# A decoder step on one core: four stores moved behind the first key evacuation, two sums of squares behind the first weight tiles

## The chip, the cores and the metric

One core of a Trainium2 chip runs the whole program. The time is device microseconds of one execution; "before" is the median of three runs. The engines are TensorE (PE, with its weight loads as PEld), VectorE (DVE), ScalarE (ACT), GpSimd (POOL) and SyncE (SP). SP issues most loads, ACT issues some loads and stores, each in the order of its own instruction stream.

## The reference, cut to what matters

The reference is one decoder layer over 512 prompt rows and 32 sample rows of width 1024: a hybrid mixer (mLSTM heads and differential attention), cross-attention to 256 memory rows, and a gated ConvFFN. The change lies in the opening, where the keys of the memory rows are made and the prompt rows are normed for the mixer's input projection:

```python
def rms_norm(x, g):
    y = xf * lax.rsqrt(jnp.mean(xf * xf, axis=-1, keepdims=True) + RMS_EPS)
    return (y * g.astype(jnp.float32)).astype(x.dtype)

def mem_kv(mem, g_mem_src, w_mk, w_mv):
    mn = rms_norm(mem, g_mem_src)
    mk = (mn @ w_mk).reshape(B, MEM_TOKENS, MEM_HEADS, MEM_HEAD_DIM)
    mv = (mn @ w_mv).reshape(B, MEM_TOKENS, MEM_HEADS, MEM_HEAD_DIM)
    return mk, mv
...
    h = rms_norm(x, g_mix_pre)
    z = h @ w_in
```

## The kernel before

**Products.** A float32 operand is split into a high part (cast to fp32r, on ACT) and a low part (the difference, on DVE or POOL: `split`, lines 146 and 147). A product is three matmuls: high x high, high x low weight, low x high weight (lines 407 to 409 for 512 columns, line 465 for the heads in two column halves). Each weight tile of 512 KB is loaded by SP into a staging buffer `wst` and split into `wslot`, of which four buffers exist. The eight tiles of `w_mk` share the low part between DVE and POOL (`split_w`, lines 221 and 223); the other tiles leave it to DVE.

**The memory rows.** Two blocks `xm` of 128 rows are loaded. `norm_turn` transposes each on PE (line 328, `tp`), multiplies it with the gain on DVE (line 330, `ht`), and splits it into `memT` (ACT line 146, POOL for the first four column tiles and DVE for the others, line 147). The row norm is not applied here: the scale 1/rms of each row (`mrs`) comes from a sum of squares on ACT (`sumsq`, line 309), two small POOL operations (`rstd`, lines 302 and 304) and a copy on DVE (line 523). It is multiplied in only when the keys leave PSUM.

**The keys.** `mem_k` makes the keys in two column halves `i`. In each, `gemmA` walks over eight tiles of 128 rows of the contraction (one step of the generator each) for both row blocks, 48 matmuls per half, and then `ev` takes each block out of PSUM: scale on ACT (line 531, `mkv`), store, four transposes on PE (line 535, `mkt`), copy and second store on ACT (lines 537 and 538). 

**The prompt rows.** The loop over `mem_k` (lines 575 to 580) puts the input norm of the five row blocks between its steps: load `xb` (line 568), sum of squares on ACT, POOL, scaling on DVE (line 318, `hN`), transposes on PE, `ht` on DVE, split into `hT` (ACT, and POOL for the first four column tiles, DVE for the others). Blocks 0 to 3 are prompt rows, block 4 the sample rows. After the keys, `gemmB` makes the four mLSTM key heads (line 465), first columns 0 to 255 (blocks 0 and 1) of all heads, then the rest, and takes them out on ACT (line 637). The gate products (lines 658 and 659) follow.

**The stores.** The products `ht` of the memory rows (`kept`, four tiles of 128 x 512) are stored to a scratch array `mem_d` by ACT (line 583), to be loaded again for the memory values (line 545, about 314 us into the span). In the text their stores stand behind the `mem_k` loop.

**What sets the order.** The text gives priorities, not the order: a scheduler orders each engine's instructions by its own estimate of when they become ready. `tc.issue_after(x)` makes what stands under it wait, in that order, for instruction `x`. The program uses eight completion counters for the DMAs of SP and ACT, given out in turn; a DMA's issue waits until the DMA eight before it, which had the same counter, has landed.

Of the kernel before, what the change touches and what calls it, by code (L numbers as in the profile page):

```python
# [15 lines left out]
P = 128  # L16
DM = 1024
# [60 lines left out]
def kernel(ctx: ExitStack, tc: tile.TileContext, I, O):  # L78
    nc = tc.nc
# [25 lines left out]
    def N(name, w=1024):  # L105
        return npool.tile([P, 1032], F32, name=name, tag="N")[:, :w]

    def T2(shape, name, dt=F32):
        return t2p.tile(list(shape), dt, name=name, tag="T2")

    def Z(name):
        return zp.tile([P, 512], F32, name=name, tag="Z")

    def at(name="at"):
        return psa.tile([P, 512], F32, name=name, tag="at")

    def mmp(name="mm"):
        return psm.tile([P, 512], F32, name=name, tag="mm")

    def small(w, name, p=P):  # L120
        return sm.tile([p, w], F32, name=name, tag=name)
# [5 lines left out]
    def v2(t, b):  # L127
        return t.rearrange("p (a b) -> p a b", b=b)
# [7 lines left out]
    VCP = nc.vector.tensor_copy  # L136
# [12 lines left out]
    def rows(b):  # L149
        return (b * P, P) if b < 4 else (SEQ, NS)  # L150
# [29 lines left out]
    xms = [N("xm") for _ in range(2)]  # L180
# [16 lines left out]
    mrs = cst.tile([P, 2], F32, name="mrs")  # L197
# [11 lines left out]
    def stage():  # L209
        return stg.tile([P, 1024], F32, name="wst", tag="st")  # L210
# [87 lines left out]
    def rstd(ss, n, w, dim, name="rs"):  # L298

        r = small(w, name)  # L300
        if dim is not None:
            nc.gpsimd.tensor_scalar(out=r[:n], in0=ss, scalar1=1.0 / dim, scalar2=EPS, op0=MUL, op1=ADD)
            ss = r[:n]
        GTT(out=r[:n], in0=ss, in1=mhalf[:n, :w], op=ALU.pow)  # L304
        return r[:n]

    def sumsq(x, n, junk, name="ssq"):
        ss = small(1, name)
        ACT(out=junk, in_=x, func=AF.Square, accum_out=ss[:n])  # L309
        return ss[:n]  # L310
# [10 lines left out]
    def norm_turn(h, n, gname, xt, c0, pool=(True, False)):  # L321

        tmps = []
        for q in range(2):
            ps = at("tp")
            pv = v2(ps, P)[:, :, :n]
            for j in range(4):
                tr(pv[:, j, :], h[:, (4 * q + j) * P:(4 * q + j + 1) * P], ident[:n, :n])
            tmp = T2([P, 4, n], "ht")
            VTT(out=tmp, in0=pv, in1=gcol(gname, 4 * q, 4 * q + 4).unsqueeze(2).broadcast_to([P, 4, n]), op=MUL)  # L330
            put(xt, q, 0, 4, c0, n, tmp, nc.gpsimd if pool[q] else None)
            tmps.append(tmp)
        return tmps

    def norm_T(x, n, gname, xt, c0):
        norm_turn(norm_rows(x, n), n, gname, xt, c0)
# [176 lines left out]
    mem_d = dram.tile([P, 8, 256], F32, name="mem_d")  # L513
# [5 lines left out]
    W.nslots = 2  # L519
    W.pump()  # L520
    kept = [norm_turn(xms[b], P, "g_mem_src", memT, b * P) for b in range(2)]
    for b in range(2):
        VCP(out=mrs[:, b:b + 1], in_=rstd(sumsq(xms[b], P, N("hN")), P, 1, DM))
    W.nslots = NSLOT
    W.pump()
    def mem_k():
        dst = O["p_mem_k"][0, 0].rearrange("t h d -> t (h d)")
        for i in range(2):
            def ev(b, ps):
                t = Z("mkv")  # L530
                nc.scalar.mul(out=t, in_=ps, mul=mrs[:, b:b + 1])
                nc.scalar.dma_start(out=dst[b * P:(b + 1) * P, 512 * i:512 * i + 512], in_=t)
                pt = at("mkt")
                for j in range(4):
                    tr(pt[:, j * P:(j + 1) * P], t[:, j * P:(j + 1) * P], ident)
                u = Z("mkT")
                nc.scalar.copy(out=u, in_=pt)
                nc.scalar.dma_start(out=mk_d[:, 4 * i:4 * i + 4, b * P:(b + 1) * P], in_=v2(u, P))
            yield from gemmA(memT, 8, [0, 1], ev)
# [26 lines left out]
    def h_in(b):  # L566
        xbs[b] = N("xb")[:rows(b)[1]]
        dma(out=xbs[b], in_=x_in(b))
# [4 lines left out]
    VTS(out=gT[:, 36:40], in0=gT[:, 36:40], scalar1=1.0 - LAM_INIT, scalar2=None, op0=MUL)  # L573
    h_in(HB[1])
    for i, _ in enumerate(mem_k()):
        if i in HSTEPS:
            j = HSTEPS.index(i)
            norm_T(xbs[HB[j]], rows(HB[j])[1], "g_mix_pre", hT, rows(HB[j])[0])
            if j + 2 < 5:
                h_in(HB[j + 2])  # L580
    for b in range(2):
        for q, t in enumerate(kept[b]):
            nc.scalar.dma_start(out=mem_d[:, 4 * q:4 * q + 4, b * P:b * P + P], in_=t)


    masks = T2([P, MASK_W], "masks")
# [67 lines left out]
    for c0, c1 in HALF:  # L654
        n = c1 - c0
        ps = mmp()
# [3 lines left out]
        t = T2([64, n], "gt")  # L660
# [47 lines left out]
    ps = at("gtp")  # L708
# [3 lines left out]
    ps = at("gtp")  # L712
# [190 lines left out]
    ps = at("npt")  # L903
# [7 lines left out]
    for g in range(2):  # L911
        for h in range(0, H, 2):
            t = stage().rearrange("p (j b e) -> p j b e", j=2, b=4)
# [27 lines left out]
    ps = at("nT0")  # L941
# [10 lines left out]
    t = None  # L952
    for h in range(H):
        with burst(t):
            t = mm(pg[NS * h:NS * h + NS, P:2 * P + 1], lhsT=sm_t[:, h, :], rhs=vNs[:, h, :], start=True, stop=True).ins
    for h in range(H):
        with burst(t):
            t = mm(pg[NS * h:NS * h + NS, 4:12], lhsT=qT[:, h, SEQ:], rhs=nT[:, h, :], start=True, stop=True).ins
    for b in range(NB):
        for h in range(H):  # L960
            with burst(t):
                t = mm(pi[NS * h:NS * h + NS, 0:P], lhsT=qzm[:, 256 * h + b * NS:256 * h + (b + 1) * NS],
                       rhs=csts[b // 4, h][:, b % 4, :], start=(b == 0), stop=(b == NB - 1)).ins
# [12 lines left out]
    ps = at("nTt")  # L976
# [317 lines left out]
    ps = at("dat")  # L1294
# [114 lines left out]
    def mk_turn(i):  # L1409
        b, c = i // 2, i % 2  # L1410
        if c == 0:
            kts[b] = wp.tile([P, 8, 256], F32, name="kT", tag="W")
        for q in range(2):
            ps = at("tpk")
            for j in range(4):
                t = tr(ps[:, j * P:(j + 1) * P], kst[i][:, (4 * q + j) * P:(4 * q + j + 1) * P], ident)
            (VCP if q else nc.scalar.copy)(out=kts[b][:, 4 * q:4 * q + 4, c * P:(c + 1) * P], in_=v2(ps, P))
        return t.ins

    def mk_scores(b):  # L1420
        ps = mmp("ssc")[:, :256]
        for c in range(2):
            for h in range(H):
                t = mm(ps[NS * h:NS * h + NS], lhsT=qs[:, 2 * h + c], rhs=kts[b][:, 2 * h + c, :], start=(c == 0), stop=(c == 1))
        sample_exp(sall, b, ps, nm, su)
        return t.ins
# [35 lines left out]
    for b in range(4):  # L1462
        t = mk_scores(b)
    with tc.issue_after(t):
        for j in range(8, 16):
            t = mk_turn(j)
# [7 lines left out]
    with tc.issue_after(t):  # L1474
        for b in range(4, NB):
            t = mk_scores(b)
# [20 lines left out]
    ps = at("ost")  # L1497
    for e in range(2):
        tr(ps[:, e * P:(e + 1) * P], oS[:, e * P:(e + 1) * P], ident)
    ps = ps[:, :256].rearrange("p (e h n) -> p h e n", e=2, n=NS)  # L1500
# [20 lines left out]
    for t0 in (0, 4):  # L1521
        ps = at("cvp")
# [5 lines left out]
    ps = at("cvp")  # L1528
# [145 lines left out]
    for gi, js in enumerate(groups):  # L1674
# [8 lines left out]
        def one(b, ps, i, s, cs=slice(0, 512)):  # L1683
            t = act[i // 2][:, i % 2]
            st, en = i == 0, i == nk - 1
            if b == 4:
                return sample_mm(ps, [acs[i], acs[i + 1]], s[1], i == 0, i == nk - 2)
            s = s[0]
            c0 = b * P
            mm(ps, lhsT=t[:, 0, c0:c0 + P], rhs=s[:, 0, i % 2, cs], start=st, stop=False)  # L1690
            mm(ps, lhsT=t[:, 0, c0:c0 + P], rhs=s[:, 1, i % 2, cs], start=False, stop=False)  # L1691
            return mm(ps, lhsT=t[:, 1, c0:c0 + P], rhs=s[:, 0, i % 2, cs], start=False, stop=en)  # L1692
# [29 lines left out]
        if not last:  # L1722
            behind = []
            for n0 in (0, 512):
# [3 lines left out]
                ps = [mmp() for _ in range(4)]  # L1728
                for i in range(nk):
# [3 lines left out]
                    for b in range(4):  # L1733
                        t = one(b, ps[b], i, s)
# [5 lines left out]
            ps = {n0: at("sdn") for n0 in (0, 512)}  # L1740
# [8 lines left out]
        def chunk(b, n0):  # L1749
            while len(wd) < (nk // 2 if n0 == 0 else nk):  # L1750
                wd.append(W.get())
            w = 256 if (b, n0) == (TORD[-1], 512) else 512
            for o in range(0, 512, w):
                ps = mmp()[:, :w]
                for i in range(0, nk, 2 if b == 4 else 1):
                    t = one(b, ps, i, wd[(n0 and nk // 2) + i // 2], slice(o, o + w))
                add_y(b, ps, n0 + o, w)
            return t
# [39 lines left out]
        t = chunk(TORD[1], 0)  # L1798

        for n0 in (0, 512):  # L1800
            with burst(t.ins):
                t = chunk(TORD[0], n0)
# [77 lines left out]
```

## Time and profile before

| what | value |
|---|---|
| median of 3 runs | 958.01 us |
| the three runs | 953.81, 958.01, 958.31 us |
| the profiled execution | 956.79 us |
| its span, first to last instruction | 955.0 us |
| its mean granted TensorE clock | 0.993 |

In the rows of the timeline the first number is the start, the second the duration, both in us; what ended the idle time before an instruction stands in brackets. "SPq" and "ACTq" are DMA issues of those engines. In a list of waits the numbers are total, times and longest. Matmuls overlap in the pipeline, so that a single 128x512 matmul lasts 0.39 us in the list while one starts every 0.23 us.

### The profile page before, as it was taken

What the parts mean: (1) busy time and instruction counts of PE and PEld (TensorE: products, weight loads), DVE (VectorE), ACT (ScalarE), POOL (GpSimd) and SP (SyncE); (2) the same over time, 40 slices, a digit from 0 to 9 for tenths busy, and PEclk for the clock granted to TensorE, in tenths of its full rate; (3) what the DMA queues carried; (4) which work ended last, traced back from release to release, by engine and by line L of the source; (5) the groups of instructions that cost most, each with busy time, mean ns of one, the idle gap of its engine ahead of it and who ended that gap; (6) DMA issues with size and microseconds to landing.
All of it is one profiled execution on the core that took longest, in us unless ns stands there. A gap on an engine that the chain in (4) does not pass through costs nothing. (4 is left out here: it accounts for less than half of the span.)

```text
span 955.0 us, 17088 instructions
## 1 busy us (share of the span) xinstructions
PE 932.7 (98%) x6619; PEld 810.6 (85%) x6619; DVE 599.2 (63%) x1129; ACT 388.8 (41%) x750; POOL 197.5 (21%) x383
## 2 busy tenths in 40 slices
PE   8999999999999999999999999999999999999995
PEld 5899777879866778998777799989988997999974
DVE  5745144565887448635654769727758676676867
ACT  5655133344676447624544523332212222222232
POOL 6610000024432217300000444001110110111114
PEclk9999999999999999999999999999999999999998
DMA  8950023334825429955953743063053302512023
GB/s 278 309 184 2 1 89 136 89 110 150 264 90 183 155 94 329 307 155 167 353 213 114 206 134 89 4 177 89 4 144 79 122 26 79 165 48 89 24 92 116
DMA packets 120674, 130.27 MB, mean 136 GB/s; under 512 B 8568, under 2 KB 86233, under 8 KB 120593
## 3 DMA queue, kind: packets, MB, share of 16 engines
q1 hardware_dynamic: 114408, 125.69, 41.9%
q10 hardware_dynamic: 6184, 3.48, 1.2%
q8 instruction: 52, 0.85, 0.4%
q14 instruction: 30, 0.24, 0.1%
HBM read 112.22 MB, written 16.93 MB: 135 GB/s over the span
## 5 line engine op out<-in xcount | busy, mean ns | idle before, releaser
L146 ACT CAST wslot<-wst 128x1024 fp32r<-128x1024 f32 x125 | 130.9, 1050 | 259.9 <-issue 74.7
L477 PE MATMUL mm<-fT,wslot 128*128 128x256 f32 x1872 | 235.9, 288 | 0.0
L477 PEld LDWEIGHTS mm<-fT,wslot 128*128 128x128 f32 x1872 | 234.4, 188 | 1.8 <-issue 0.8
L147 DVE TENSOR_TENSOR wslot<-wst,wslot 128x1024 fp32r<-128x1024 f32 x125 | 155.1, 1245 | 89.3 <-ACT wslot L146 88.8
L1691 PE MATMUL mm<-wslot,act 128*128 128x512 f32 (+1 forms) x180 | 70.2, 391 | 0.0
L1692 PE MATMUL mm<-wslot,act 128*128 128x512 f32 (+1 forms) x180 | 70.0, 392 | 0.0
L1690 PE MATMUL mm<-wslot,act 128*128 128x512 f32 (+1 forms) x180 | 69.3, 387 | 0.0
L1598 POOL COPY cvo<-u 128x2 f32<-128x2 f32 x43 | 11.0, 256 | 204.8 <-DVE u L1596 194.7
L407 PE MATMUL mm<-wslot,hT 128*128 128x512 f32 x128 | 52.2, 408 | 0.0
L409 PE MATMUL mm<-wslot,hT 128*128 128x512 f32 x128 | 51.5, 403 | 0.0
L408 PE MATMUL mm<-wslot,hT 128*128 128x512 f32 x128 | 51.3, 401 | 0.0
L477 PE MATMUL mm<-hT,wslot 128*128 128x256 f32 (+1 forms) x384 | 51.0, 289 | 0.0
L1593 DVE TENSOR_TENSOR u<-mm,rsb 128x256 f32<-128x256 f32 x43 | 18.2, 424 | 51.0 <-PE mm L477 50.1
L477 PEld LDWEIGHTS mm<-hT,wslot 128*128 128x128 f32 x384 | 49.2, 188 | 0.5 <-issue 0.2
L1690 PEld LDWEIGHTS mm<-wslot,act 128*128 128x128 f32 x180 | 34.3, 191 | 8.0 <-issue 0.8
L1691 PEld LDWEIGHTS mm<-wslot,act 128*128 128x128 f32 x180 | 33.8, 188 | 7.2
L1692 PEld LDWEIGHTS mm<-wslot,act 128*128 128x128 f32 x180 | 33.8, 188 | 7.2 <-issue 0.4
L1610 ACT ACTIVATE c<-c 128x560 f32<-128x560 f32 x21 | 14.1, 672 | 56.7 <-DVE c L1604 56.7
L1604 DVE SCALAR_TENSOR_TENSOR c<-u,cvT,c 128x560 f32<-128x560 f32 x43 | 34.3, 798 | 0.9
L1603 DVE SCALAR_TENSOR_TENSOR c<-u,cvT,c 128x560 f32<-128x560 f32 x43 | 34.1, 793 | 0.2
L1703 DVE TENSOR_TENSOR yp<-mm,yp 128x512 f32<-128x512 f32 (+1 forms) x41 | 27.2, 674 | 5.1 <-PE mm L1692 5.0
L409 PEld LDWEIGHTS mm<-wslot,hT 128*128 128x128 f32 x128 | 24.5, 191 | 5.3
(474 smaller groups left out, 1857.7 us busy)
## 6 DMA issues: line engine op xcount, KB each, us to landing
wst<-in_w_up_dram SPq DMA_DIRECT2D x42, 512.0 KB
wst<-in_w_in_dram SPq DMA_DIRECT2D x28, 512.0 KB
wst<-in_w_down_dram SPq DMA_DIRECT2D x20, 512.0 KB
wst<-in_cache_mem_k_dram SPq DMA_DIRECT2D x16, 512.0 KB
wst<-in_w_mk_dram SPq DMA_DIRECT2D x8, 512.0 KB
xb<-in_x_prompt_dram SPq DMA_DIRECT2D x8, 512.0 KB
wst<-in_cache_dk_dram SPq DMA_DIRECT2D x16, 256.0 KB
wst<-in_cache_dv_dram SPq DMA_DIRECT2D x16, 256.0 KB
```

Source lines behind the costliest of these rows:

```text
L146: nc.scalar.copy(out=hi, in_=src)
L147: (eng or nc.vector).tensor_tensor(out=lo, in0=src, in1=f32(hi), op=SUB)
L407: mm(ps[b], lhsT=xt.hi(k, c0, c0 + n), rhs=s[:, 0, kk, :], start=(k == 0), stop=False)
L408: mm(ps[b], lhsT=xt.hi(k, c0, c0 + n), rhs=s[:, 1, kk, :], start=False, stop=False)
L409: return mm(ps[b], lhsT=xt.lo(k, c0, c0 + n), rhs=s[:, 0, kk, :], start=False, stop=(k == nk - 1))
L477: mm(ps[i], lhsT=s[:, l, k, :], rhs=x(k, c0, c1), start=(k == 0 and j == 0), stop=(k == 7 and j == 2))
L1603: STT(out=c, in0=u[:, 1:EXT - 1], scalar=w[1], in1=c, op0=MUL, op1=ADD)
L1604: STT(out=c, in0=u[:, 0:EXT - 2], scalar=w[0], in1=c, op0=MUL, op1=ADD)
L1690: mm(ps, lhsT=t[:, 0, c0:c0 + P], rhs=s[:, 0, i % 2, cs], start=st, stop=False)
L1691: mm(ps, lhsT=t[:, 0, c0:c0 + P], rhs=s[:, 1, i % 2, cs], start=False, stop=False)
L1692: return mm(ps, lhsT=t[:, 1, c0:c0 + P], rhs=s[:, 0, i % 2, cs], start=False, stop=en)
L1703: VTT(out=y, in0=ps, in1=y, op=ADD)
```

## The change

The sums of squares of the memory rows, with what makes `mrs` of them, go into a function that is called in the loop over `mem_k` at step 3, half-way through the first column half. The four stores to `mem_d` keep their place in the text and now wait for the second evacuation of `mem_k` (block 1 of the first column half).

```diff
     kept = [norm_turn(xms[b], P, "g_mem_src", memT, b * P) for b in range(2)]
-    for b in range(2):
-        VCP(out=mrs[:, b:b + 1], in_=rstd(sumsq(xms[b], P, N("hN")), P, 1, DM))
     W.nslots = NSLOT
     W.pump()
+    def mem_rms():
+        for b in range(2):
+            VCP(out=mrs[:, b:b + 1], in_=rstd(sumsq(xms[b], P, N("hN")), P, 1, DM))
+    evm = []
...
-                nc.scalar.mul(out=t, in_=ps, mul=mrs[:, b:b + 1])
+                evm.append(nc.scalar.mul(out=t, in_=ps, mul=mrs[:, b:b + 1]))
...
     for i, _ in enumerate(mem_k()):
+        if i == 3:
+            mem_rms()
         if i in HSTEPS:
...
-    for b in range(2):
-        for q, t in enumerate(kept[b]):
-            nc.scalar.dma_start(out=mem_d[:, 4 * q:4 * q + 4, b * P:b * P + P], in_=t)
+    with tc.issue_after(evm[1].ins):
+        for b in range(2):
+            for q, t in enumerate(kept[b]):
+                nc.scalar.dma_start(out=mem_d[:, 4 * q:4 * q + 4, b * P:b * P + P], in_=t)
```

The scheduler makes a new order of it on all five engines. Lines behind the change are numbered up to 9 higher (535 for 531, 539 for 535, 592 for 583). First ACT, at the splits of the memory rows; `memT0` is the high part of the turned rows, `wslot_119` the first weight tile, `ht` the turned rows times the gain. Before:

```order
L221 CAST wslot_119<-wst_118 128x1024
L146 CAST memT0_138<-ht_136 128x4x128
L583 DMA mem_d_115<-ht_136 128x4x128
L146 CAST memT0_138<-ht_147 128x4x128
L309 ACTIVATE hN_176,ssq_177<-xm_90 128x1024
L583 DMA mem_d_115<-ht_147 128x4x128
L146 CAST memT0_138<-ht_156 128x4x128
L221 CAST wslot_126<-wst_125 128x1024
L583 DMA mem_d_115<-ht_156 128x4x128
L146 CAST memT0_138<-ht_165 128x4x128
```

And with the change:

```order
L221 CAST wslot_119<-wst_118 128x1024
L146 CAST memT0_138<-ht_136 128x4x128
L146 CAST memT0_138<-ht_147 128x4x128
L221 CAST wslot_126<-wst_125 128x1024
L146 CAST memT0_138<-ht_156 128x4x128
L146 CAST memT0_138<-ht_165 128x4x128
L221 CAST wslot_170<-wst_169 128x1024
```

The stores and the sums have left, and the second tile (`wslot_126`) is now cast ahead of block 1 (`ht_156`, `ht_165`). POOL follows: its half of `wslot_126` stands ahead of the low part of block 1, where the two small operations of the sum stood.

Second PE, from the last key product to the first head products; `tp_292` and `tp_301` are the transposes of block 1, `tp_349` and `tp_358` of block 2, `hT00` and `hT10` the high and low part of the first four column tiles of the normed rows, `mm_577` and `mm_603` the first two heads. Before (rows that repeat are left out):

```order
L328 MATMUL tp_301<-cpk_87,hN_285 128x128 x4
L409 MATMUL mm_392<-wslot_337,memT1_139 128x512
L465 MATMUL mm_577<-hT00_244,wslot_406 128x256
L465 MATMUL mm_577<-hT10_245,wslot_406 128x256
L328 MATMUL tp_349<-cpk_87,hN_342 128x128 x4
L328 MATMUL tp_358<-cpk_87,hN_342 128x128 x4
L535 MATMUL mkt_372<-cpk_87,mkv_369 128x128 x4
```

With the change:

```order
L409 MATMUL mm_392<-wslot_337,memT1_139 128x512
L328 MATMUL tp_292<-cpk_87,hN_285 128x128 x4
L328 MATMUL tp_301<-cpk_87,hN_285 128x128 x4
L328 MATMUL tp_349<-cpk_87,hN_342 128x128 x4
L328 MATMUL tp_358<-cpk_87,hN_342 128x128 x4
L539 MATMUL mkt_372<-cpk_87,mkv_369 128x128 x4
L465 MATMUL mm_577<-hT00_230,wslot_406 128x256
L465 MATMUL mm_603<-hT00_230,wslot_448 128x256
L465 MATMUL mm_577<-hT10_231,wslot_406 128x256
```

The transposes of block 1 have gone from among the key products to behind them, next to those of block 2 and ahead of the first head product, which reads both blocks 0 and 1.

Third ACT, around the same place; `wslot_492` and `wslot_509` are the eleventh and twelfth weight tile, `xb_310` the rows of block 3, `xb_367` the sample rows, `ht_297` and `ht_306` block 1. Before:

```order
L146 CAST hT00_244<-ht_297 128x4x128
L146 CAST wslot_448<-wst_447 128x1024
L309 ACTIVATE hN_342,ssq_343<-xb_259 128x1024
L146 CAST wslot_492<-wst_491 128x1024
L146 CAST hT01_255<-ht_306 128x4x128
L309 ACTIVATE hN_410,ssq_411<-xb_310 128x1024
L146 CAST wslot_509<-wst_508 128x1024
```

With the change:

```order
L146 CAST wslot_492<-wst_491 128x1024
L146 CAST wslot_509<-wst_508 128x1024
L309 ACTIVATE hN_410,ssq_411<-xb_310 128x1024
L309 ACTIVATE hN_458,ssq_459<-xb_367 32x1024
L146 CAST hT00_230<-ht_297 128x4x128
L146 CAST hT01_241<-ht_306 128x4x128
L541 COPY mkT_377<-mkt_372 128x512
L535 ACTIVATE mkv_380<-mm_197,mrs_112 128x512
L592 DMA mem_d_115<-ht_136 128x4x128
```

The casts of block 1 stand behind the twelfth tile and two sums now, and the first store behind `mkv_380`, the second evacuation. Behind the gate products each engine's order is the one before.

## Prediction

> **What bounds the kernel now.** I read the page first: one core, and TensorE (PE) is busy almost all the time.
>
> ```profile
> span 955.0 us, 17088 instructions
> PE 932.7 (98%) x6619; PEld 810.6 (85%) x6619; DVE 599.2 (63%) x1129; ACT 388.8 (41%) x750; POOL 197.5 (21%) x383
> ```
>
> So a change that removes no matmul gains only where PE stands still. Where that is, and for whom, says the list of waits of PE, which also has the two waits of the later input norm.
>
> ```profile
> PE mm L409 <- POOL memT L147: 1.2, 2, 0.6
> PE tp L328 <- DMA xm<-in_mem_prompt_dram: 1.0, 1, 1.0
> PE tp L328 <- DVE hN L318: 0.9, 2, 0.6
> ```
>
> These are the only waits of the opening that are not the warm-up: 3.1 us. Third, the table by stage, cut at the first key product (9.46), at the first product of the mLSTM key heads (35.44) and at the first gate product (65.34). Its columns are the stretch, then busy time (and instructions) of PE, weight loads, DVE, ACT and POOL, granted clock, DMA share, GB/s.
>
> ```profile
> 9.46:14.00 4.54, 3.31 (x15) 2.16 (x14) 4.41 (x7) 3.15 (x6) 4.37 (x5) 1.00 0.96 331
> 14.00:35.44 21.44, 21.44 (x104) 17.54 (x102) 16.57 (x17) 14.06 (x19) 17.06 (x15) 1.00 0.96 312
> 35.44:65.34 29.90, 28.93 (x234) 28.34 (x233) 16.22 (x29) 16.93 (x33) 9.25 (x17) 1.00 0.76 216
> ```
>
> In the middle stretch the DMA engines are 96% busy and DVE and POOL about 80%, but PE does not wait at all: the loads are ahead of it. The stores that the change moves run in just this stretch. They do hurt one engine, SP, whose queue stood 4.6 us behind a store (the small gain loads of L167 reuse its completion counter):
>
> ```profile
> SPq L167 <- DMA mem_d<-ht: 4.6, 1, 4.6
> 17.63 0.27 SPq L167 DMA_DIRECT2D grow<-in_g_ffn_pre_dram  x1
> 8.35 0.47 ACTq L583 DMA_DIRECT2D mem_d<-ht  x1
> ```
>
> The store issued at 8.35 released SP only at 17.63, 9.3 us later. But the full PE of 14.00 to 35.44 says that nobody on the path paid for it.
>
> The built orders differ on all five engines up to the gate products, and not behind them. So the whole effect is the sum of PE's stalls up to 65.34, and it then moves the rest of the program as one block: PE is the bound there, and I count the shift one to one.
>
> **First products of the keys: about 0.** On ACT, two sums of squares of 1.06 us and four issues leave this place.
>
> ```profile
> 6.71 1.05 ACT L221 CAST wslot<-wst 128x1024 fp32r<-128x1024 f32 x1 [0.20 <-DMA wst<-in_w_mk_dram]
> 9.38 1.06 ACT L309 ACTIVATE hN<-xm 128x1024 f32<-128x1024 f32 x1
> 7.83 1.27 POOL L223 TENSOR_TENSOR wslot<-wst,wslot 128x512 fp32r<-128x512 f32 x1 [0.60 <-ACT wslot L221]
> 9.06 1.72 POOL L147 TENSOR_TENSOR memT<-ht,memT 128x512 fp32r<-128x512 f32 x1
> 10.84 0.50 PE L409 MATMUL mm<-wslot,memT 128*128 128x512 f32 x1 [0.64 <-POOL memT L147]
> 10.87 0.52 POOL L302 TENSOR_SCALAR rs<-ssq 128x1 f32<-128x1 f32 x1
> 11.47 0.56 POOL L304 TENSOR_TENSOR rs<-rs,mhalf 128x1 f32<-128x1 f32 x1
> 13.34 0.50 PE L409 MATMUL mm<-wslot,memT 128*128 128x512 f32 x1 [0.59 <-POOL memT L147]
> ```
>
> The first sum ended before the weight tile had landed (the cast at 6.71 waited for its DMA), so the chain cast 6.71, POOL half 7.83, POOL memT 9.06, PE 10.84 stays: wait of 0.64 kept. The wait for xm (1.0) stays too, since SP's first loads keep their order. The second wait, 0.59 at 13.34, loses what stood before it on POOL (0.52 and 0.56, 10.87 to 12.03) and gets a weight half of 1.27 (its row above) in that place, since POOL now takes `wslot_126` before block 1's low half. PE meanwhile does six products of the second tile first. Bounds: the whole 0.59 gained, or, with the POOL half at 1.72 like its neighbour, some 0.7 lost. I take 0. In the later key products PE waited nowhere (21.44 of 21.44), so lighter DMA brings nothing there.
>
> **The sums behind the first tiles: 0.** They are still 2 x 1.06 on ACT, two pairs on POOL and two small copies on DVE, and now stand ahead of block 1's rows in the norm chain (ACT sum, POOL, DVE hN). PE asks for that hN only after the last key product. Without an earlier start that would be up to half a us too late; the loads, without the 4.6 us hold of SP, come up to that much earlier. I take 0, and 0.5 for the range.
>
> **The hand-over from key products to heads: +2.3.** This is where the order has really changed. All transposes of blocks 1 and 2 now come after the last key product; before, block 1's stood among the products.
>
> ```profile
> 25.43 1.03 PE L328 MATMUL tp<-cpk,hN 128*128 128x128 f32 x8
> 26.22 0.71 PE L407 MATMUL mm<-wslot,memT 128*128 128x512 f32 x2
> 35.44 1.59 PE L465 MATMUL mm<-hT,wslot 128*128 128x256 f32 x12
> 37.67 1.07 PE L328 MATMUL tp<-cpk,hN 128*128 128x128 f32 x8 [0.65 <-DVE hN L318]
> 38.57 0.60 PE L535 MATMUL mkt<-cpk,mkv 128*128 128x128 f32 x4
> 38.93 4.67 PE L465 MATMUL mm<-hT,wslot 128*128 128x256 f32 x35
> 48.66 0.65 PE L328 MATMUL tp<-cpk,hN 32*128 32x32 f32 x8 [0.30 <-DVE hN L318]
> 37.42 1.05 ACT L309 ACTIVATE hN<-xb 128x1024 f32<-128x1024 f32 x1
> 38.48 1.03 ACT L146 CAST wslot<-wst 128x1024 fp32r<-128x1024 f32 x1
> 45.66 1.06 ACT L309 ACTIVATE hN<-xb 32x1024 f32<-32x1024 f32 x1 [1.82 <-DMA xb<-in_x_sample_dram]
> 41.37 0.62 ACT L146 CAST hT<-ht 128x512 fp32r<-128x512 f32 x1 [1.85 <-DVE ht L330]
> 30.59 3.99 POOL L147 TENSOR_TENSOR hT<-ht,hT 128x512 fp32r<-128x512 f32 x2
> 48.93 1.29 POOL L147 TENSOR_TENSOR hT<-ht,hT 128x512 fp32r<-128x512 f32 x1 [1.22 <-ACT hT L146]
> ```
>
> Call E the end of the last key product; eight transposes take 0.79 (25.43 to 26.22), so E is 35.44 - 0.79 = 34.65. PE then has 16 transposes (1.58) and 4 of mkt (38.57 to 38.93, 0.36): 1.94 of work. The first product of the heads needs block 1's hT from ACT, where four things stand in its way: the cast of the twelfth tile (`wslot_509`), which may start only at E because its buffer is the one that the last key products read, then the sums of block 3 and of the sample rows, then the cast itself: 1.05 + 1.06 + 1.06 + 0.62 = 3.79. First wait: 3.79 - 1.94 = 1.85. Then PE has two products, and the third wants POOL's low half: 1.29 to 2.00 (half of 3.99), I take 1.6 for a POOL beside a busy DVE. A product takes 0.13 (4.67 over 35), so the second wait is 1.6 - 0.26 = 1.34. Together 3.2, in place of the 0.65 and 0.30 that PE waited for hN: +2.25. Bounds: -0.95, if ACT turns out to be in time, and +4, if POOL takes 2.0 and ACT is held by a load (below).
>
> **The stores: 0.** Their four issues, 0.37 to 0.61 us each, now stand on ACT behind the second key evacuation, among the casts of block 2.
>
> ```profile
> L583 ACTq DMA_DIRECT2D mem_d<-ht x4: 367/438/607, 8.3 to 13.9; - x4
> ```
>
> PE has some 12 us of first-half products then (4 heads x 24 x 0.13) that need blocks 0 and 1 alone; if that cover were gone, 4 x 0.44 = 1.8 would show. Their buffers are not needed by the casts of blocks 1 and 2, and memory values are read much later.
>
> The sum: 0 + 0 + 2.25 + 0 on the profiled execution, 956.79 (span 955.0 and 1.8 around it), gives 959.0. That execution lies 0.1% under the median of the three runs (958.01), inside their spread of 953.81 to 958.31, so 959.0 is also my time for the median. About 0.5%, 4.8 us, is what a measurement of this kernel can tell from no change.
>
> **Rivals.**
>
> *No wait at the hand-over.* If ACT and POOL reach block 1 in time (shorter queue than I read off the order), the 0.95 goes and perhaps the 0.59: 955.3 to 956.8. For it: the loads come earlier, so ACT may do the two sums before E. Against it: the twelfth cast cannot start before E, and they stand behind it. 18%.
>
> *ACT held by the stores: slower.* A load on ACT (the masks, L596) reuses the counter of the first store, as SP's did, and the second counter is asked for right after it. Behind them on ACT stands the last key evacuation, whose transposes PE wants when the heads' first half is nearly done, 12 us after about 40: at 52. With the 9.3 us of the row at 8.35, a store issued near 41 lands at 50.3, ACT needs some 3 us for what is queued, and PE waits 1.3. The point from which it decides is a counter free only after 51.6; at 52.5 PE would wait 3.5, which makes 959.0 + 3.5 = 962.5. For it: four mem_d stores, the first key stores and four weight loads now meet in a stretch that was full already (DMA share 1.10, in the row's last column but one):
>
> ```profile
> 40.00:45.00 5.00, 5.00 (x46) 5.00 (x45) 3.76 (x5) 2.48 (x5) 2.45 (x2) 1.00 1.10 279
> ```
>
> Against it: SP's loads come earlier and leave that stretch sooner. 8%.
>
> *Block 3's rows late.* The sum of block 3 on ACT waits for a load that now follows two weight tiles more on SP.
>
> ```profile
> 30.27 0.34 SPq L568 DMA_DIRECT2D xb<-in_x_prompt_dram  x1
> ```
>
> Before, they were issued at 30.27 and in use at 37.42; the changed ACT asks for them at 35.7. Each us later costs one: landing at 37.4 as now gives 959.0 + 1.7 = 960.7, and over 38.3 it is more than 0.5%. 10%.
>
> *The clock falls in the wait.* PE ran at clock 1.00 in all three stretches, through single waits of 0.65. Two waits of 3.2 us with two products between are longer than any wait of this opening behind the warm-up; if the array then ran at half speed for as long as it waited, 3.2 us of products would take 1.6 more: 960.6. 6%. [...]
>
> **How the numbers follow.** The forecast, a hand-over wait of 2 to 4 us, has 58%. Its own range is 957 to 961. The range goes down to the no-wait case less the spread of runs, 954.5, and up to just past 962.5, the decisive end of the two held-ACT cases: 963.0. Slower by over 0.5%: 5% of the store rival, the far part of the row rival (4%), 1% of the rest: 10%. Faster by over 0.5% is out of reach of PE's waits (3.1 us in all, 1.64 of them kept); 4% for run spread. Within: 86%.
>
> **What would show it.** After: PE waits of about 1.9 for an ACT cast of hT and 1.3 for POOL's hT at 36 to 40 us, two sums of squares just before that cast; no wait of SP for a store near 13 us; the first gate product at 67.6 (65.34 + 2.25); nothing different behind it. It is wrong if the gate product starts before 65.3, if PE waits in the key products, or if the span moves by more than the gate product does.

## The result, and the profile after

The change makes the kernel slower. Six executions of the changed kernel have a median of 964.89 us (962.91 to 967.31), six of the kernel before, beside them, 958.16 (953.81 to 961.43): a ratio of 1.007, with a 95% interval of 1.005 to 1.009. Measured again later (e13 below) it was 966.39 against 956.98, ratio 1.0095 (1.0071 to 1.0118). The prediction said 959.0, no change; the range ended at 963.0.

The page of the changed kernel, at the same two lines:

```profile
span 961.1 us, 17100 instructions
PE 935.3 (97%) x6619; PEld 812.9 (85%) x6619; DVE 598.9 (62%) x1129; ACT 388.1 (40%) x750; POOL 196.3 (20%) x383
```

The profiled execution took 962.91 us, 6.1 us more than that of before. The same 6619 matmuls take PE 2.6 us more, and it stands still 3.5 us longer (25.8 us in place of 22.3). Where, the table by stage says. It is cut, behind the first two cuts of the table before, at the end of the key products (36.63), at the third head product, from which PE runs on without a break (44.14), behind the lowered clock (48.00) and at the first gate product (72.84); columns as before, the clock is the third number from the end.

```profile
9.46:14.00 4.54, 4.00 (x13) 2.87 (x12) 3.79 (x5) 2.90 (x4) 4.04 (x4) 0.52 1.02 390
14.00:36.63 22.63, 22.63 (x99) 18.38 (x98) 16.58 (x20) 15.28 (x22) 17.98 (x19) 0.95 1.01 303
36.63:44.14 7.51, 3.26 (x23) 2.36 (x21) 5.93 (x8) 6.35 (x11) 4.44 (x6) 0.97 0.76 196
44.14:48.00 3.86, 3.86 (x21) 3.86 (x22) 2.57 (x4) 0.34 (x2) 1.71 (x2) 0.61 1.11 373
48.00:72.84 24.84, 24.84 (x200) 24.50 (x198) 8.55 (x16) 10.16 (x20) 3.73 (x10) 1.00 0.44 136
72.84:961.00 888.16, 870.69 (x6250) 757.96 (x6248) 558.45 (x1071) 349.18 (x686) 161.63 (x335) 1.00 0.41 127
```

Three things differ. The first products run at clock 0.52, behind a wait of 2.1 us ahead of the turn of the second memory block. The profile names DVE's half of the first weight tile as what ended it; in other traces (e8, 2.1 us; e13, 1.7) the same wait ends with the landing of that block's rows.

```profile
9.01 1.38 PE L328 MATMUL tp<-cpk,xm 128*128 128x128 f32 x8 [2.08 <-DVE wslot L223]
```

Between keys and heads PE works 3.26 of 7.51 us. Behind that the clock is at 0.61 for 3.86 us. The first gate product is 7.5 us later than in the trace of before (65.34), the span only 6.1 longer. The rest is 1.5 us shorter, and the reason is in before: a spell of half clock behind a run of very small matmuls, which the changed kernel's trace doesn't have. The rows are of the kernel before, from its first gate product on, and in that spell:

```profile
65.34:955.00 889.66, 872.26 (x6250) 758.85 (x6248) 558.74 (x1071) 349.56 (x686) 162.81 (x335) 0.99 0.41 127
95.80:99.20 3.40, 3.40 (x16) 2.34 (x16) 0.48 (x3) 0.00 (x0) 0.00 (x0) 0.54 0.00 0
```

Now the hand-over, in the changed kernel's timeline: PE first, then ACT, then POOL.

```profile
36.63 1.47 PE L328 MATMUL tp<-cpk,hN 128*128 128x128 f32 x12
38.33 0.66 PE L328 MATMUL tp<-cpk,hN 128*128 128x128 f32 x4 [0.23 <-DVE ht L330]
39.02 0.63 PE L539 MATMUL mkt<-cpk,mkv 128*128 128x128 f32 x4
41.00 0.51 PE L465 MATMUL mm<-hT,wslot 128*128 128x256 f32 x2 [1.35 <-ACT hT L146]
44.14 2.08 PE L465 MATMUL mm<-hT,wslot 128*128 128x256 f32 x8 [2.64 <-POOL hT L147]
```

```profile
36.87 1.05 ACT L146 CAST wslot<-wst 128x1024 fp32r<-128x1024 f32 x1 [1.67 <-PE mm L409]
38.25 1.06 ACT L309 ACTIVATE hN<-xb 128x1024 f32<-128x1024 f32 x1 [0.33 <-DMA xb<-in_x_prompt_dram]
39.30 1.04 ACT L309 ACTIVATE hN<-xb 32x1024 f32<-32x1024 f32 x1
40.34 0.60 ACT L146 CAST hT<-ht 128x512 fp32r<-128x512 f32 x1
```

```profile
39.48 0.57 POOL L302 TENSOR_SCALAR rs<-ssq 128x1 f32<-128x1 f32 x1 [4.86 <-ACT hN L309]
40.11 0.95 POOL L658 MEMSET wgs<- 128x1024 f32 x1
41.03 0.55 POOL L304 TENSOR_TENSOR rs<-rs,mhalf 128x1 f32<-128x1 f32 x1
41.66 0.75 POOL L302 TENSOR_SCALAR rs<-ssq 32x1 f32<-32x1 f32 x1
42.49 1.60 POOL L147 TENSOR_TENSOR hT<-ht,hT 128x512 fp32r<-128x512 f32 x1
```

The chain is the predicted one: twelfth weight tile, two sums, block 1's cast. But the sum of block 3 waits for its load (0.33; the other traces below have 1.39 and 4.15). SP issues that load 1.7 us later than in the trace of before (30.27):

```profile
32.01 0.35 SPq L572 DMA_DIRECT2D xb<-in_x_prompt_dram  x1
```

And POOL, which was free from 34.6 on, does not take block 1's low half when the cast is done at 40.94: it is busy with block 3's and the sample rows' `rstd` and with clearing the gate weights (`wgs`), until 42.49. So the waits are 0.23, 1.35 and 2.64, 4.2 us.

### The profile page after: what moved, and what is told of

Same layout as the page of the kernel before. It is cut to its first block, busy times and chain, and to the rows that moved or that the text cites. A ratio compares the mean times of both kernels' runs of the same rounds, so it can differ in the third digit from the quotient of the medians.

```text
span 961.1 us, 17100 instructions
## 1 busy us (share of the span) xinstructions
PE 935.3 (97%) x6619; PEld 812.9 (85%) x6619; DVE 598.9 (62%) x1129; ACT 388.1 (40%) x750; POOL 196.3 (20%) x383
## 5 line engine op out<-in xcount | busy, mean ns | idle before, releaser
L477 PE MATMUL mm<-hT,wslot 128*128 128x256 f32 (+1 forms) x384 | 51.0, 289 | 0.0
L1612 DVE SCALAR_TENSOR_TENSOR c<-u,cvT,c 128x560 f32<-128x560 f32 x43 | 34.1, 793 | 0.2
L465 PE MATMUL mm<-hT,wslot 128*128 128x256 f32 (+1 forms) x192 | 27.3, 301 | 4.0 <-POOL hT L147 2.6
```

The lines of the kernel that those rows point to most:

```text
L465: mm(ps, lhsT=s[:, l, k, :], rhs=x(k, c0, c1), start=(k == 0 and j == 0), stop=(k == 7 and j == 2))
L477: mm(ps[i], lhsT=s[:, l, k, :], rhs=x(k, c0, c1), start=(k == 0 and j == 0), stop=(k == 7 and j == 2))
L1612: STT(out=c, in0=u[:, 1:EXT - 1], scalar=w[1], in1=c, op0=MUL, op1=ADD)
```

## The experiments

Theory 1: the loss is the hand-over, whose order arises from the two moves together. Theory 2: one of the moves costs by itself. Theory 3: the half clock at the first products is chance. Theories 1a and 1b ask whether a lowered clock costs time or only accompanies a wait. Times are medians; each ratio is against executions of the kernel before on the same chip.

**e1, the sums alone.** The stores stand in the text as before:

```diff
-    with tc.issue_after(evm[1].ins):
-        for b in range(2):
...
+    for b in range(2):
```

> Only the sums are moved; the stores stand as in the kernel before. In the order of this kernel block 1's transposes stand among the key products again, 16 products ahead of the last. Theory 1 (the loss is the hand-over from keys to heads, where both row blocks are turned late and PE waits for ACT and POOL, with the lowered clock behind such waits): those 4 us of waits do not arise, the granted clock stays at 1.00 from 35 to 60 us, and the time is that of before within 3 us, 956 to 961. Theory 2 (moving the sums costs by itself, by holding the row buffers longer): most of the 6.7 us, 962 to 966. Theory 3 (the half clock at the first products is chance, not the change): tells nothing of the time; whether this trace has it at 9 to 16 us is one more draw.

**e2, the stores alone.** The sums go back to their old place, `issue_after` stays.

> Only the stores are moved; the sums stand as in the kernel before. Block 1's transposes stand among the key products in this order too. Theory 1 (hand-over): no long wait of PE between the last key product and the heads, 956 to 961. Theory 2 (the stores' new place costs, by what they meet in the DMA queues and on ACT): PE waits for a cast or for rows behind 40 us, 962 to 966. Theory 3 as in the first run: one more draw of the clock at the first products.

Measured: e1 959.52 against 957.26, ratio 1.0016 (0.9999 to 1.0033); e2 959.16, ratio 1.0015 (0.9997 to 1.0033). From 20 to 80 us the list of PE's waits has one row in e1, among the keys, and two in e2. First e1, then e2:

```profile
PE mm L408 <- DVE wslot L223: 1.2, 1, 1.2
```

```profile
PE tp L328 <- ACT mkT L538: 1.3, 1, 1.3
PE mkt L536 <- ACT mkv L532: 0.4, 1, 0.4
```

The two losses together, some 4 us at their medians, are less than the 6.7 of both moves, and neither can be told from none. In its trace e2 also lost time at the start, with a wait of 3.1 us for the second memory block and 6.8 us of half clock, so that the place of its loss is not settled by the two rows. As theory 2 had it, one move alone would bring most of the loss; it does not. Block 1's late turn, which only the pair brings, is left as the main suspect.

**e3, zeros in the waits.** Matmuls on zeros keep PE busy in both gaps, behind the last transpose of the first memory block (`ltr`) and behind the first four `mkt` transposes (`lmk`):

```diff
+    with tc.issue_after(ltr[0].ins):
+        for _ in range(8):
+            mm(wp2, lhsT=warm[:, 0:P], rhs=warm, start=True, stop=True)
...
+                        with tc.issue_after(lmk[3].ins):
+                            for _ in range(30):
+                                mm(ps, lhsT=warm[:, 0:P], rhs=warm[:, :c1 - c0], start=True, stop=True)
```

> The changed kernel with matmuls on zeros put where PE waits: 8 of 128x512 between the turns of the two memory blocks (1.7 us where PE stood idle for 2.1), and 30 of 128x256 ahead of the first head product (3.2 us, where it waited 1.35 and 2.64). The waits stay, only the clock is kept up. Theory 1a (half of the loss is the lowered clock: 13 first products at half speed, and the head products from 44 to 47 us): granted clock 1.00 from 9 to 60 us, key products end 1.5 to 3 us earlier than 36.6, first gate product at 67.5 to 70 in place of 72.8, time 960 to 963. Theory 1b (the waits alone cost, the clock is no more than their sign): gate product at 72 to 73, time 964 to 967, or more if the added matmuls stand in the way.

Measured 964.29, ratio 1.0064 (1.0038 to 1.0089). At the start the clock stayed at 1.00 and the keys ended at 35.34, 1.3 us earlier; no time came of it. At the hand-over the experiment failed: the clock fell to 0.50 behind a wait of 1.9 ahead of the zeros, which then took 4.8 us and held the heads up.

**e4, the queues mended.** The norms of block 3 and of the sample rows wait for block 1's cast, clearing `wgs` waits for its low half; the first line stands for the blocks from the fourth on:

```diff
+                with tc.issue_after(cast1.ins):
+                    norm_T(xbs[HB[j]], rows(HB[j])[1], "g_mix_pre", hT, rows(HB[j])[0])
...
+    with tc.issue_after(low1.ins):
+        nc.gpsimd.memset(wgs, 0.0)
```

> The changed kernel with its order mended at the hand-over alone: the input norms of block 3 and of the sample rows (their sums on ACT) are issued behind the cast of block 1's rows, and the clearing of the gate weights on POOL behind block 1's low half. Theory 1 (queues of ACT and POOL make the hand-over wait): the wait for the ACT cast goes from 1.35 to under 0.3, the one for POOL's low half from 2.64 to 1.3 to 1.6 (its own duration less two products), and the clock stays up there, so 2.5 to 4.5 us come back: 960 to 962.5; what stays is the slow start. Theory 2 (something else, such as DMA or the stores, holds the hand-over): the waits stay at some 4 us in sum under other names, 964 to 966.

Measured 961.7, ratio 1.0045 (1.0028 to 1.0062); the waits are 3.0 us:

```profile
36.85 1.47 PE L332 MATMUL tp<-cpk,hN 128*128 128x128 f32 x12
39.98 0.66 PE L332 MATMUL tp<-cpk,hN 128*128 128x128 f32 x4 [1.67 <-DVE ht L334]
42.84 3.41 PE L469 MATMUL mm<-hT,wslot 128*128 128x256 f32 x15 [1.30 <-POOL hT L149]
```

The wait for the ACT cast is gone and that for POOL has halved; the one for DVE (block 1's `ht` behind two weight splits) was 0.23 in the first trace of the changed kernel and is now the longest. The queues are a cause, and a third of the loss by the medians, though the intervals of this run and of the changed kernel (1.005 to 1.009) overlap. The clock did fall again (0.63 from 42 to 44 us).

**e5, the sums at step 5; e6, the same with the zeros at the start.**

```diff
-        if i == 3:
+        if i == 5:
             mem_rms()
```

> The changed kernel, stores and all, with the sums of the memory rows called at step 5 of the loop in place of step 3, that is behind the input norm of block 1 in place of ahead of it. In its order block 1's transposes stand among the key products again, 12 products ahead of the last, and 43 head products follow on the keys without a break. Theory 1 (the loss lies in the hand-over, and comes from the place of the sums ahead of block 1 together with the stores): no PE wait over 1 us from 34 to 50 us, clock 1.00 there, first gate product at 66 to 69, time 955 to 960.5. Theory 2 (the two moves cost by themselves): 962 to 966 as in the changed kernel.

> As the run with the sums at step 5, and with 8 matmuls of 128x512 on zeros between the turns of the two memory blocks, where PE stands idle for 1.8 to 3.1 us and the clock fell to half in four of six traces. Theory 1a (the half clock at the first products costs time): clock 1.00 from 9 to 18 us, 1 to 2 us under the same kernel without them, 954 to 959. Theory 1b (PE has slack there, since the weight tiles come no faster than products at half speed eat them): no difference from the kernel without them within 1 us.

Measured: e5 962.4, ratio 1.0043 (1.0026 to 1.006); e6 963.44, ratio 1.0058 (1.0038 to 1.0078). Block 1 is turned among the keys here, and theory 1 as first put falls: that alone does not mend it. In e5 PE waits twice over a us behind 34 us:

```profile
37.66 5.26 PE L465 MATMUL mm<-hT,wslot 128*128 128x256 f32 x42 [1.13 <-POOL hT L147]
54.59 2.67 PE L465 MATMUL mm<-hT,wslot 128*128 128x288 f32 x17 [1.51 <-ACT hT L146]
```

The two moved sums now stand on ACT at 33.83 and 35.92, one ahead of block 1's casts, and the `rstd` of the first on POOL ahead of its low half; everything behind them is late too. So the theory becomes wider: in the 10 us ahead of the heads the blocks' own sums, casts and low halves come due just in time, and whatever is put ahead of them is paid for. (e11 tests this for POOL; for ACT it is argued.) In e6 the clock stayed at 1.00 at the start and the keys ended 1.2 us earlier than in e5 (35.10 and 36.26), but the time did not fall, as in e3: theory 1b at the start.

**e7, the kernel before with the zeros at the start; e8, the kernel before again,** one execution for its trace.

> The kernel before with the same 8 matmuls between the turns. Theory 3 (the half clock at the first products is met by the kernel before as well, in most of its executions, so that it is no part of the 0.7%): the time falls by 0.5 to 2 us, ratio 0.998 to 0.9995. If the kernel before is never halved there, the matmuls do nothing or delay: ratio 1.000 to 1.002.

> The kernel before once more, for its trace. Theory 3 (chance): half clock at 9 to 16 us as in the changed kernel, with a wait of 1.8 us or more for the second memory block. If the half clock came from the change, this trace has clock 1.00 there as the first one had.

e7: 959.32, ratio 1.0025 (1.0006 to 1.0044), no gain, rather a loss: the products then wait 1.4 us for weight casts and 1.0 for a low half. e8: 953.59, span 951.8, and half clock at the first products, in the kernel before:

```profile
PE tp L328 <- DMA xm<-in_mem_prompt_dram: 2.1, 1, 2.1
```

```profile
9.00:10.00 1.00, 1.00 (x6) 0.50 1.04 385
```

So this spell is not the change's, and here it costs next to nothing: the heads start at 35.6, and at 35.44 in the first trace of before, which has no spell but 1.2 us of waits for POOL's `memT` at this place. Theory 3 holds.

**e9, the sums at step 1.** In the order they go back among the first weight tiles; the stores stay late.

> The changed kernel with the sums of the memory rows called at step 1 of the loop, ahead of all input norms; in its order they stand among the casts of the first weight tiles (ahead of and behind the second), as in the kernel before, and the stores stay behind the second key evacuation. Refined theory 1 (what costs is the sums' work on ACT and POOL in the stretch ahead of the heads, where the row blocks' own sums, casts and low halves are due just in time): 956.5 to 960.5, gate product at 64.5 to 68, no wait over 1 us from 34 to 56. Theory 2 (the stores in their new place cost, and the run with the stores alone was lucky): 961 to 965.

Measured 960.63, ratio 1.0028 (1.001 to 1.0047): less than half of the loss, just above what was expected; the gate product, at 68.9, is 0.9 above. PE waits 1.0 and 0.7 us for ACT's `mkv` and `mkT`, near 43 and 48, as in e2. ACT issues the stores there; whether those issues or the other work in its queue makes it late was not separated.

**e10, the changed kernel again,** one execution, and **e13, again with timing,** for two more draws.

> The changed kernel once more, for its trace. Theory 1: waits of PE for ACT and POOL at the hand-over (36 to 45 us) of 3.5 to 4.7 us in sum, with half clock behind them, gate product at 71 to 74, whatever the clock does at the first products. Theory 3 (chance in that trace): the hand-over waits under 2 us.

> The changed kernel again, timed next to the run with zeros at the hand-over: 963 to 966, ratio 1.005 to 1.009, and a third trace of its hand-over: waits of 3.5 to 5.5 us in sum at 36 to 45 us with 3 to 11 us of half clock behind them.

e10 took 968.28. Both traces go beyond what was expected: the gate product comes at 74.7 and 74.5, and the waits of e13 add up to 7.4 us. First e10's rows of PE and of ACT, then those of e13 and two rows of its table by stage:

```profile
39.10 0.66 PE L328 MATMUL tp<-cpk,hN 128*128 128x128 f32 x4 [1.69 <-DVE ht L330]
41.37 0.79 PE L465 MATMUL mm<-hT,wslot 128*128 128x256 f32 x2 [0.75 <-ACT hT L146]
44.91 4.64 PE L465 MATMUL mm<-hT,wslot 128*128 128x256 f32 x20 [2.75 <-POOL hT L147]
...
38.62 1.06 ACT L309 ACTIVATE hN<-xb 128x1024 f32<-128x1024 f32 x1 [1.39 <-DMA xb<-in_x_prompt_dram]
```

```profile
34.75 1.47 PE L328 MATMUL tp<-cpk,hN 128*128 128x128 f32 x12
37.76 0.66 PE L328 MATMUL tp<-cpk,hN 128*128 128x128 f32 x4 [1.54 <-DVE ht L330]
42.94 0.80 PE L465 MATMUL mm<-hT,wslot 128*128 128x256 f32 x2 [3.86 <-ACT hT L146]
45.71 4.10 PE L465 MATMUL mm<-hT,wslot 128*128 128x256 f32 x20 [1.98 <-POOL hT L147]
...
40.19 1.06 ACT L309 ACTIVATE hN<-xb 128x1024 f32<-128x1024 f32 x1 [4.15 <-DMA xb<-in_x_prompt_dram]
```

```profile
34.75:45.71 10.96, 3.55 (x23) 2.57 (x22) 7.23 (x10) 6.36 (x11) 4.07 (x6) 0.84 0.82 242
45.71:50.00 4.29, 4.29 (x24) 4.29 (x25) 2.58 (x4) 0.34 (x2) 1.72 (x2) 0.62 1.10 374
```

Side by side, with the two traces of before (all in us; half clock is counted from the granted clock in windows of 2 us, between the last key product and the gate):

| trace | keys end | block 3 lands | waits at the hand-over | third head product | half clock | gate product |
|---|---|---|---|---|---|---|
| changed | 36.63 | 38.25 | 4.2 | 44.14 | 3.4 | 72.84 |
| e10 | 35.94 | 38.62 | 5.2 | 44.91 | 10.2 | 74.7 |
| e13 | 34.75 | 40.19 | 7.4 | 45.71 | 6.8 | 74.5 |
| before | 35.44 | - | 0.95 | 35.7 | 0 | 65.34 |
| e8 (before) | 35.6 | - | 0 | 35.8 | 0 | 64.1 |

The end of the keys moves by 1.9 us in the three changed traces and the third head product does not follow it. It follows block 3's load: 5.9, 6.3 and 5.5 us behind its landing, that is, two sums, a cast and POOL's queue. (In the kernel before, the third head product is two products behind 35.44.) In the first trace two things were late together: the keys ended at 36.63, so that ACT was through with the twelfth tile at 37.92, 0.33 us ahead of the landing. In e10 and e13 it stood 1.39 and 4.15 us for the landing. The load was issued at 32.01, 32.48 and 33.55 and landed 6.1 to 6.6 us later; what makes it so late was not tested. Nor does it explain e3, where the sum of block 3 began at 36.69 and the zeros themselves ran on until the first head product at 44.71.

**e11, the kernel before with POOL held up.** Clearing the low half again and again puts the wait into the kernel before (`c` is the block's cast, 11 times in all):

```diff
+        if held and eng is not None:
+            with tc.issue_after(c.ins):
+                for _ in range(held.pop()):
+                    nc.gpsimd.memset(f32(lo), 0.0)
```

> The kernel before with one cost added: POOL clears the low half of blocks 0 and 1 eleven times more (some 0.5 us each, 9 of them between block 0's low half and block 1's), so that the first head products wait for POOL as in the changed kernel; sums and stores stand as before. Refined theory 1 (a hand-over wait costs what it lasts, and 1.2 to 1.7 us more when the clock falls behind it): PE waits 3 to 4.5 us for POOL between 35 and 42, gate product at 68.5 to 71, time 961 to 965, ratio 1.003 to 1.008. Theory 4 (PE waits there are made up later, since the loads or ACT bound the heads' second half anyway): gate product within 1.5 us of 64.1 to 65.3 and ratio under 1.002.

Measured 961.38, ratio 1.0034 (1.0014 to 1.0053), gate product at 70.6. The waits come out at 3.7 us, under the name of DVE but on the chain behind POOL's queue (the `rstd` of block 2 stands among the clears), with 6.8 us of half clock from 39.5 on:

```profile
38.23 1.06 PE L334 MATMUL tp<-cpk,hN 128*128 128x128 f32 x8 [2.47 <-DVE hN L324]
41.06 1.12 PE L541 MATMUL mkt<-cpk,mkv 128*128 128x128 f32 x4 [1.26 <-DVE ht L336]
```

Theory 4 falls: such waits are not made up later. They cost 3.2 us at the medians.

**e12, zeros at the hand-over alone,** 10 inside the transposes of block 2 and 20 ahead of the heads, timed beside e13.

> The changed kernel with matmuls on zeros at the hand-over alone: 10 of 128x256 (1.1 us) inside the transposes of block 2, where PE waited for DVE, and 20 (2.1 us) ahead of the first head product. The waits for ACT and POOL stay, but PE is busy in most of them. If the half clock behind the waits is a part of the loss of its own: clock 1.00 from 36 to 56 us, and from the first head product to the first gate product 1.2 to 3.5 us less than in the two traces of the changed kernel (31.8 and 33.3 us); time 1 to 3 us under the changed kernel. If the waits alone set the time: no difference, or up to 1 us more, where the zeros stand in the way.

Measured 963.17, ratio 1.0075 (1.005 to 1.0099), where e13 had 1.0095 (1.0071 to 1.0118): lower, but the intervals overlap. The trace is clearer. Rows of the table by stage up to the third head product and behind it:

```profile
36.48:44.44 7.96, 5.96 (x54) 5.30 (x52) 6.78 (x9) 6.33 (x11) 3.79 (x6) 1.00 0.81 224
44.44:48.00 3.56, 3.56 (x31) 3.56 (x32) 2.94 (x5) 0.95 (x4) 1.72 (x2) 1.00 1.10 374
```

The clock stays at 1.00, and from the third head product to the gate it takes 27.4 us (44.44 to 71.8). The three changed traces take 28.7, 29.8 and 28.8. So in these traces the lowered clock costs 1.3 to 2.4 us of its own, and the waits the rest.

**e14, block 3's rows loaded twice.** A load more, into the same place; the order, made anew, puts the sum of these rows behind the casts of blocks 1 and 2.

```diff
-        dma(out=xbs[b], in_=x_in(b))
+        for _ in range(2 if b == 3 else 1):
+            dma(out=xbs[b], in_=x_in(b))
```

> The changed kernel with block 3's rows loaded twice into the same place, a load more. The order is made anew with these rows counted as later: their sum, and that of the sample rows, now stand behind the casts of blocks 1 and 2 on ACT, and POOL clears the gate weights behind their low halves. The three traces of the changed kernel have the third head product 5.5 to 6.3 us behind the landing of block 3's rows (38.25, 38.62, 40.19), whenever the keys ended (36.63, 35.94, 34.75). If the casts of block 1 behind these rows on ACT are what holds the hand-over: no wait of the hand-over for a cast that stands behind this landing, waits there of under 3 us in sum, and a time 2 to 5 us under the changed kernel (960 to 963), although a load is added. If the late loads as such cost (DMA bandwidth): slower than the changed kernel, 966 to 969.

Measured 962.74 against 958.96, ratio 1.0048 (1.0026 to 1.0069). First PE, then ACT:

```profile
37.35 0.66 PE L328 MATMUL tp<-cpk,hN 128*128 128x128 f32 x4 [1.48 <-DVE ht L330]
40.20 2.88 PE L465 MATMUL mm<-hT,wslot 128*128 128x256 f32 x22 [1.29 <-POOL hT L147]
50.37 1.09 PE L328 MATMUL tp<-cpk,hN 128*128 128x128 f32 x8 [1.75 <-DVE hN L318]
```

```profile
47.46 1.06 ACT L309 ACTIVATE hN<-xb 128x1024 f32<-128x1024 f32 x1 [5.94 <-DMA out_dram<-mkv]
```

The third head product comes at 40.20, 4 to 5.5 us earlier than in the changed traces, with a load more, and the clock stays at 1.00. So it was the queue behind the landing, not the load as such. Part is lost again: ACT stands 5.94 us ahead of block 3's sum, and block 3 is late for the second half. The profile names the landing of a store there; but the second load of block 3 was issued only at 40.77, and with the 6.1 to 6.6 us of its forerunners it lands at about 47 (an estimate), so that either may have held ACT. The median is 2.2 to 3.6 us under those of the changed kernel; the interval is clear of that of e13 (1.0071 to 1.0118) and overlaps the first (1.005 to 1.009).

No version tried beats the kernel before, so none is proposed. Two ends stay open: where the 2 us by which each move alone is slower at the median go, if they are real, and what makes block 3's load land late.

## Why the prediction was wrong

*The hand-over, +2.25: the step that failed, by its size.* The place, the order of ACT's queue and both releasers were right. But "together 3.2" was 4.2, 5.2 and 7.4, and the first gate product, put at 67.6, came at 72.84, 74.7 and 74.5. Three things were missing in the sum, and the runs price each:

- Block 3's load. The prediction let ACT reach the sum of block 3 at 35.7 and find the rows there; their lateness was a rival, "each us later costs one". They landed at 38.25, 38.62 and 40.19, which is 2.55, 2.9 and 4.5 later. (On SP the load follows three weight tiles more than before, six of `w_in` in place of three, not two.)
- POOL's queue. The second wait was taken as the low half's own duration, 1.6 - 0.26 = 1.34. It was 2.64, 2.75 and 1.98, 1.3, 1.4 and 0.6 more, since `rstd` operations and the clearing of `wgs` stood ahead. The order of POOL was not read at this place as that of ACT was.
- The clock. The rival "the clock falls in the wait" had 6% and +1.6. It came true in all three changed traces, and in e3, e4 and e11; it costs 1.3 to 2.4 (e12). The 1.6 was the author's estimate, from a half clock that lasts as long as the waits. The runs do not bear it out: behind waits of 4.2, 5.2 and 7.4 us the three traces have 3.4, 10.2 and 6.8 us of it. What went ahead of the fall was short: in the first trace waits of 1.35 and 2.64 us with two products between (it fell at 43.75), in e10 one of 1.69 us among the transposes (it fell at 40.08, ahead of the first head product). And the trace of before has the spell at 95.80, which the prediction did not use.

Put into the prediction's own sum these give, for the three traces, 959.0 + 2.55 + 1.3 + 1.3 = 964.2, 959.0 + 2.9 + 1.4 + 2.4 = 965.7 and 959.0 + 4.5 + 0.6 + 1.4 = 965.5. These executions took 962.91, 968.28 and 966.96, and the medians are 964.89 and 966.39. At the gate product, where nothing behind it mixes in, the same terms give 67.6 + 5.15 = 72.7, 67.6 + 6.7 = 74.3 and 67.6 + 6.5 = 74.1, against 72.84, 74.7 and 74.5. The wait for DVE's `ht` (0.23, 1.69, 1.54) was not foreseen either; it lies in time in which ACT's queue holds the heads anyhow. That the keys ended at 36.63 in place of E = 34.65 is no fourth term: the rows landed later still, though in this trace by 0.33 us only, so that rows in time would have gained no more there.

*The chances.* The two rivals that came true had 10% and 6% and were priced one at a time, as if one shut the other out. They lie on the same chain and add up. In the first trace no single term, and not even these two together (959.0 + 2.55 + 1.3 = 962.9), leaves a range that ended at 963.0; it takes POOL's queue as well, which was no rival. In e13 block 3's load alone does it (963.5).

*First products of the keys, 0: not shown wrong.* The half clock there was not foreseen. It belongs to no version (e8 has it, e10 has not). In the changed kernel the keys ended 2.0, 1.3 and 0.1 us behind E, but the heads waited for block 3's load in each; that this cost nothing is thus luck, and no merit of the working. In e10 PE waits 2.0 us for POOL's `memT` at the first products, in place of 1.2; the larger part stands at the first of the two waits (1.28 for 0.64), which the prediction took as kept.

*The sums, 0, and the stores, 0: not shown wrong.* Alone they have 1.0016 and 1.0015, intervals that just reach 1; the stores late with the sums early (e9) have 1.0028, which does not. The held-ACT rival may have come true at small size: there are waits of 0.4 to 1.3 us for ACT in e2 and e9, and one of 1.75 us for block 3's rows behind a late ACT in e14, but whether the stores made ACT late was not separated.

*"It then moves the rest of the program as one block."* By and large: 7.5 us at the gate, 6.1 in the span. The prediction took the reverse, a span that moves by more than the gate product, as a sign of error; the gap comes from the half clock spell at 95.80 in one trace of before, 1.6 us that another trace (e8) doesn't have.

## What to carry to other kernels

Where an engine waits for a chain through several queues, read what stands ahead of the awaited instruction on every one of them, and ask of each of these when its own input lands: one load waited for in order on ACT set the start of all heads here, in two of three traces by more than a microsecond on its own. Rivals that lie on the same chain are not alternatives; add them up before setting the range. One trace of each kernel is one draw: the second and third trace told which differences belong to the change.

## What the runs showed of the hardware

The lowered clock comes in spells of 3.4 us or whole multiples: 3.4, 6.8 and 10.2 in the sixteen traces, by windows of the granted clock from 4 to 140 us. Windows of 0.25 us give the moments at which it falls, in the changed kernel's first trace and in e13:

```profile
9.50:9.75 0.25, 0.25 (x4) 0.73 1.05 393
43.50:43.75 0.25, 0.00 (x0) 0.99 1.13 336
```

```profile
8.00:8.25 0.25, 0.00 (x0) 0.60 0.89 262
42.00:42.25 0.25, 0.00 (x0) 0.86 0.48 117
```

A clock of 0.73 in the first, with the lowered clock at 0.50 (9.75 to 16 us), means full speed for 0.115 of its 0.25 us. So it falls at 9.61 and at 43.75, 34.1 us apart, ten of the shortest spells; in e13 at 8.05 and 42.18, 34.1 again. No length of a wait shows as the limit: a wait of 2.1 us was enough in e8 and in the changed kernel, in e12 the clock fell at 13.55 behind two waits of 0.6, and in the kernel before it fell at 96.1 with PE counted as busy throughout, behind 1.9 us of matmuls on 4 rows each. In e8 the same small matmuls, from about 92.7 to 94.5 (an estimate: e8's gate product is 1.2 us earlier than that of before), did not make it fall (1.00 from 92 to 100). How much work keeps the clock up, and what sets these two traces apart, was not found. With 8 matmuls on zeros in the gap (e3, e6, e7) no trace had it at the first products (1.00 from 4 to 22 us in all three).

Of the wait of SP for a store, the trace of before shows this: the store issued at 8.35 is the fourteenth DMA that SP and ACT issue, and the gain load that waited 4.6 us for it and was issued at 17.63 is the twenty-second, eight later.
